# Attention with gate projections woven in: an output's addition ordered directly behind its copy, and the first gate's second half accumulated in the output's bank

## The chip, the core and the metric

The kernel runs on one core of one Trainium2 chip. The metric is the time of one execution on the device in microseconds; the median of several executions counts. Beside it there is one profiled execution, from which all rows of the trace in this document come. The engines are called as the profile calls them: PE is TensorE's matmuls, PEld its weight loads, DVE is VectorE, ACT is ScalarE, POOL is GpSimd, SP is SyncE.

## The reference

One transformer block over 1024 tokens of width 1024, in float32. The input is normalized and modulated, and one wide projection gives queries, keys and values of 8 attention heads, the streams of a recurrent branch (RWKV-7), and two gates of 1024 columns. Attention has a causal mask and a decay that is summed along the sequence:

```python
logits = einsum('bhqd,bhkd->bhqk', q, k) * scale + cum[..., :, None] - cum[..., None, :]
probs  = softmax(where(causal, logits, -inf))
o_fox  = einsum('bhqk,bhkd->bhqd', probs, v)
gate_fox, gate_rwkv = split(sigmoid(p_gate), 2, axis=-1)
merged = gate_fox * (o_fox @ fox_w_out) + gate_rwkv * (o_rwkv @ rwkv_w_out)
h = h + gate1 * (merged @ w_o)
```

A second half of the block, a gated feed-forward network with a short convolution, and a last normalization follow. The change touches only the stretch in which attention is computed, together with the last part of the gate projection `p_gate`.

## The kernel before

The work runs in stages: modulation and normalization, the recurrent branch with the projections beside it, attention, the two branch projections, the output projection, and the feed-forward network. To keep nearly float32 precision, a large product is done as three products of values that are split into a high and a low part (`hi`, `lo`).

**The planner.** In the recurrent stage and in attention the order of TensorE's instructions is written out by a small planner in Python, `Weave`. It keeps a clock of its own, `weave.now`, in nanoseconds, which every matmul advances by a fixed cost (a gate matmul of 512 columns costs 512 / 2.4 = 213), and one clock for ScalarE and one for VectorE, which `use(engine, after, cost)` advances. The work that matters is written as chains (generators) that issue instructions and then yield how long to wait. `run` takes the chain that is due, with spawned chains first. If none is due, `fill` issues matmuls of the filler, one at a time, until the next chain is due. The filler of the attention stage are the late gates: of the 16 gate tiles of 128 columns, those that are left when attention begins. While `weave.hold` lies ahead of the clock, no filler is issued.

In this stage the orders on TensorE, VectorE and ScalarE are the order in which the chains issue the instructions. Each of these engines works through its queue in that order, waiting where an operand isn't ready. The queues of SP and POOL, which carry the weight loads, the casts of late weights to their high part, and the loads of the heads, are ordered by the tile framework.

**Attention.** `s_chain` begins at 10,500 on the planner's clock, when the first head is expected to be loaded; until then only filler is issued. For a head `h` and a pair of row blocks `I` it issues logits into bank pairs `lg`. `softmax` takes the negated maximum (VectorE, line 1049), the exponential with its sum (ScalarE, 1053), the reciprocal and the scaling (VectorE, 1058 and 1059). `t_chain` transposes the probabilities (`tp`), `halve` splits them into `th` (ScalarE, 1086) and `tl` (VectorE, 1089), and `a_chain` multiplies them by the values into `ov_ps`, half of the only output bank. The high and the low part of the values give two halves of 64 rows there.

**`collect`** empties the output bank, once for every head and `I`, 32 times. ScalarE copies one half of the rows (line 1120). The chain yields until the planner's clock is past that copy, and only then is VectorE's addition of the other half issued (line 1122). So whatever other chains issue on VectorE in between comes ahead of the addition. `ov_free` then tells `a_chain` when the bank is free again.

**`late_gate`** issues a gate tile as two halves of 512 columns, 24 matmuls each, both into the one bank `rk_ps`. After a half it sets `weave.hold` and spawns `gate_out`, which reads the bank twice on ScalarE (Abs and Relu, lines 1162 and 1163), sets the hold anew to the planned end of these, and finishes the sigmoid in SBUF with two more activations, an addition and an exponential (1165 to 1170). The second half of the last gate stays in the bank and is read out after the stage.

Of the kernel before, what the change touches and what calls it, by code (L numbers as in the profile page):

```python
# [9 lines left out]
F32 = mybir.dt.float32  # L10
F32R = mybir.dt.float32r
AF = mybir.ActivationFunctionType
# [6 lines left out]
NH = 512  # L19
# [113 lines left out]
def hybrid_block(ctx: ExitStack, tc: tile.TileContext, a, out):  # L133
    nc = tc.nc
    weave = Weave()
    ctx.enter_context(tc.manual_schedule(engines={mybir.EngineType.PE}))

    def mm(o, lhsT, rhs, start, stop, more=False):

        weave.mm_cost(o, lhsT, rhs)  # L140
        nc.tensor.matmul(o, lhsT, rhs, start=start, stop=stop, skip_group_check=more)  # L141
# [5 lines left out]
    def f32(ap):  # L147
        return ap.bitcast(F32)
# [95 lines left out]
    marks = {}  # L244
    late_lo = deque()

    def lower(wait=0):

        yield wait
        if late_lo:  # L250
            hi, lo, raw = late_lo.popleft()
            for c in range(0, 1024, NH):
                tt(lo[:, c : c + NH], raw[:, c : c + NH], f32(hi[:, c : c + NH]), op=ALU.subtract)
            weave.use("DVE", weave.now, 1300)
# [30 lines left out]
    def gemm_steps(ps, w, x, cs, nk=KT, w0=0, by_kt=False):  # L285
        (wh, wl), (xh, xl) = w, x
        order = [(i, kt) for i in range(3) for kt in range(nk)]
        if by_kt:
            order.sort(key=lambda o: o[1])
        for n, (i, kt) in enumerate(order):  # L290
            ww, xx = ((wh, xh), (wh, xl), (wl, xh))[i]
            k0 = (w0 + kt) * 128
            mm(ps, ww[:, k0 : k0 + 128], xx[:, kt, cs], start=n == 0, stop=n == len(order) - 1)
            yield
# [27 lines left out]
    u = (u_hi, u_lo)  # L322
# [4 lines left out]
    def gate_steps(w, i, pps, ptag, pool, tag):  # L327
        if weave.late == 1:
            yield from late_gate(w, i)
            return  # L330
        for hf in range(2):
            cs = slice(hf * NH, hf * NH + NH)
            ps = pps.tile([128, NH], F32, tag=ptag, name=f"gt{i}_{hf}")
            yield from gemm_steps(ps, w, u, cs)

            g = pool.tile([128, NH], F32, tag=tag, name=f"gs{i}_{hf}")
            nc.scalar.activation(g, ps, AF.Abs)
            nc.scalar.activation(g, g, AF.Exp, scale=-1.0)
            nc.scalar.activation(g, g, AF.Ln, bias=1.0)
            stt(g, ps, 0.0, g, op0=ALU.min, op1=ALU.subtract)  # L340
            nc.scalar.activation(g, g, AF.Exp)
            nc.sync.dma_start(d_gate[i, :, cs], g)


    pb = ctx.enter_context(tc.tile_pool(name="pb", bufs=2, space=PS))
    with ExitStack() as es:
# [66 lines left out]
        with tc.tile_pool(name="st", bufs=1) as st, tc.tile_pool(name="stp", bufs=2, space=PS) as stp, \  # L413
# [24 lines left out]
            def mod_load(i, tags):  # L438
                ws = [st.tile([128, D], F32, tag=tags[kt % len(tags)], name=f"wm{i}{kt}", bufs={"mw": 4, "xt": 8}[tags[kt % len(tags)]])
                      for kt in range(KT)]  # L440
                for kt, w in enumerate(ws):
                    nc.sync.dma_start(w, a["w_mod"][kt * 128 : kt * 128 + 128, i * D : i * D + D])
                return ws, st.tile([128, D], F32, name=f"acc{i}")
# [69 lines left out]
            m = [mod_load(1, ("mw",)), None]  # L513
# [496 lines left out]
    with tc.manual_schedule(engines={mybir.EngineType.DVE, mybir.EngineType.Activation}):  # L1010
        seq = [(h, I) for h in range(8) for I in ((0, 1, 3, 2) if h == 7 else (3, 0, 2, 1))]
        lg_free, tp_free, pl_free, ps_free, th_free, ov_free = (deque([0.0] * n) for n in (2, 2, 4, 2, 3, 1))
        probs, av_queue, halves = {}, deque(), {}
        ov_ps = pb.tile([128, NH], F32, tag="big", name="ov")[:, 0:256]
        rk_ps = pb.tile([128, NH], F32, tag="big", name="rk_ps")

        def slot(free):
# [76 lines left out]
        def a_chain():  # L1094

            for _ in range(8 * 10):
                while not av_queue:
                    yield 100
                t, h, I, jj, th, tl = av_queue.popleft()
                yield t - weave.now  # L1100
                if jj == 0:
                    yield from slot(ov_free)
                vh = heads[h][2]
                order = [(0, th), (1, th), (1, tl), (0, tl)] if jj == I else [(0, th), (0, tl), (1, th), (1, tl)]
                for x, (k, t) in enumerate(order):
                    o0 = 128 if (jj == I and k == 1) else 0
                    mm(ov_ps[:, o0:256], vh[:, 2 * jj + k, :], t[:, 256 * k : 256 * k + 256 - o0],
                       start=jj == 0 and x == 0, stop=jj == I and x == 3)
                th_free.append(weave.now + 260)
                if jj == I:  # L1110
                    weave.spawn(collect(h, I), 260)
                yield 0

        def collect(h, I):
            p, hf, oc = h // 2, I // 2, slice(I % 2 * 256, I % 2 * 256 + 256)
            rows = slice(h % 2 * 64, h % 2 * 64 + 64)
            if (p, hf) not in halves:
                halves[p, hf] = at.tile([128, NH], F32, tag="o", name=f"o{p}{hf}"), []
            o, got = halves[p, hf]
            nc.scalar.copy(o[rows, oc], ov_ps[rows, :])  # L1120
            yield weave.use("ACT", weave.now, 270) + 140 - weave.now
            tt(o[rows, oc], o[rows, oc], ov_ps[64 - h % 2 * 64 : 128 - h % 2 * 64, :], op=ALU.add)
            t = weave.use("DVE", weave.now, 340) + 140
            ov_free.append(t + 70)
            got.append(I)
            if len(got) == 4:
                cs = slice(hf * NH, hf * NH + NH)
                if h < 7:
                    nc.gpsimd.tensor_copy(fx[0][p][:, cs], o)
                    nc.gpsimd.tensor_tensor(fx[1][p][:, cs], o, f32(fx[0][p][:, cs]), op=ALU.subtract)  # L1130
                    return
                yield t - weave.now
                nc.scalar.copy(fx[0][p][:, cs], o)
                yield weave.use("ACT", weave.now, 530) + 140 - weave.now
                tt(fx[1][p][:, cs], o, f32(fx[0][p][:, cs]), op=ALU.subtract)
# [4 lines left out]
        def late_gate(w, i):  # L1140
            while any(x[1] is w[1] for x in late_lo):
                for _ in lower():
                    pass
            for hf in range(2):
                cs = slice(hf * NH, hf * NH + NH)
                yield from gemm_steps(rk_ps, w, u, cs)
                if i == 15 and hf == 1:

                    marks["rest"] = rk_ps
                    return  # L1150
                weave.hold = weave.now + 1000
                pending.append((i, hf))
                weave.spawn(gate_out(i, hf, cs), 260)
                yield

        def gate_out(i, hf, cs):

            n = marks["gate"] = marks.get("gate", 0) + 1
            g = (at.tile([128, NH], F32, tag="gs", name=f"gs{i}_{hf}", bufs=1) if n % 3 == 1 else
                 gsp.tile([128, NH], F32, tag="sp0", name=f"gs{i}_{hf}"))  # L1160
            m = at.tile([128, NH], F32, tag="gm", name=f"gm{i}_{hf}", bufs=1)
            nc.scalar.activation(g, rk_ps, AF.Abs)
            nc.scalar.activation(m, rk_ps, AF.Relu, scale=-1.0)
            weave.hold = weave.use("ACT", weave.now, 960) + 210
            nc.scalar.activation(g, g, AF.Exp, scale=-1.0)
            nc.scalar.activation(g, g, AF.Ln, bias=1.0)
            yield weave.use("ACT", weave.now, 960) + 140 - weave.now
            tt(g, g, m, op=ALU.add)
            yield weave.use("DVE", weave.now, 600) + 140 - weave.now
            nc.scalar.activation(g, g, AF.Exp, scale=-1.0)  # L1170
            weave.use("ACT", weave.now, 480)
            nc.sync.dma_start(d_gate[i, :, cs], g)
            pending.remove((i, hf))
# [12 lines left out]
    def bank(k, name):  # L1186
        return pb.tile([128, NH], F32, tag="big", name=name) if k > 5 else pz.tile([128, NH], F32, tag=f"p{k}", name=name)
# [34 lines left out]
    if "rest" in marks:  # L1222
        g, m = (gsp.tile([128, NH], F32, tag="sp0", name=f"rest{k}") for k in range(2))
        i = nc.scalar.activation(g, marks["rest"], AF.Abs)
# [405 lines left out]
    ps = {t: [bank(k, f"wo{t}_{c}") for c, k in enumerate(ks)] for t, ks in enumerate(((0, 5), (6, 7), (1, 2)))}  # L1630
# [12 lines left out]
    def wo_do(t, k):  # L1643
        ps = [bank(k + c, f"wo{t}_{c}") for c in range(2)]
        for kt in range(KT):
            wo_mm(t, kt, ps)
        return ps

    ps = wo_do(3, 3)
# [7 lines left out]
    ps = wo_do(4, 0)  # L1657
# [15 lines left out]
    for t, k in ((5, 2), (6, 6), (7, 4)):  # L1673
        ps = wo_do(t, k)
# [229 lines left out]
    for s, k in enumerate(ORDER):  # L1904
        ps = banks[4:] if k in (7, 4, 2) else banks[0:4]
        own = NP - 4 if s == 6 else NP
        for j in range(own):
            u = s * NP + j
# [106 lines left out]
```

## Time and profile before

| | |
|---|---|
| Runs | 1660.62, 1658.31, 1658.08 us; median 1658.31 |
| Profiled execution, its own time | 1662.01 us |
| Span from its first to its last instruction | 1660.2 us |
| Mean granted TensorE clock | 0.989 |
| Gate matmuls into `rk_ps` | from 622.4 us on |
| First and last addition of `collect` (line 1122) | 653.4 and 827.4 us |
| First matmuls of the branch projections | 829.09 us |

A row of the trace gives start and duration in microseconds, the engine, the line, the operation, the tile written and the tiles read (buffer numbers left out), the shape, and the number of instructions merged in the row. In brackets stands how long the engine was idle before it, and whose end released it. Most matmuls have line 141 and most transposes line 145, since helpers issue them; they are told apart by their tiles. A row of a table by stretch gives the busy time of each engine in that stretch and the granted clock, 1.00 being full speed.

### The profile page before, as it was taken

The page shows a single profiled execution, that of the slowest core. Times are in us where ns is not written, and L with a number is a line of the kernel's source. Part 1 is how long each engine was busy: PE and PEld are TensorE (multiplying, and loading weights), DVE is VectorE, ACT ScalarE, POOL GpSimd, SP SyncE. Part 2 cuts the span into 40 slices and gives each one's busy share as a digit, 9 for nine tenths or more (in the row PEclk, how much of TensorE's full clock was granted, in tenths as well). Part 3 has the DMA queues.
Part 4 walks back from the last instruction along what each step waited for, and adds up shares of the span by engine and source line. Part 5 has one row for each costly group of instructions (what it writes and reads, how often), then busy time and mean ns, then how long its engine had stood idle before and what let it go on. Part 6 is the DMA issues. An engine that isn't in the chain of part 4 may idle for free.

```text
span 1660.2 us, 25947 instructions
## 1 busy us (share of the span) xinstructions
PE 1615.2 (97%) x9694; PEld 1346.1 (81%) x9694; DVE 1223.2 (74%) x2371; ACT 822.3 (50%) x1540; POOL 130.3 (8%) x152
## 2 busy tenths in 40 slices
PE   7999999999999999999999999999999999999998
PEld 7777777898978788888778887888888888888886
DVE  5786787878876536888678347897777777786677
ACT  5563335444455656666623225654444444555455
POOL 0011001111111011221022000000000000000000
PEclk9999999999999999999999999999999999999999
DMA  8488645443343246433187411243223223574363
GB/s 336 139 322 238 177 116 140 131 121 97 100 115 97 96 129 153 124 114 110 64 323 265 166 70 58 66 138 108 96 95 120 97 96 108 208 266 156 125 209 108
DMA packets 121645, 240.59 MB, mean 145 GB/s; under 512 B 40048, under 2 KB 48880, under 8 KB 121520
## 3 DMA queue, kind: packets, MB, share of 16 engines
q1 hardware_dynamic: 113040, 220.58, 40.7%
q0 software_dynamic: 8480, 18.37, 4.2%
q8 instruction: 76, 1.25, 0.3%
q14 instruction: 49, 0.40, 0.1%
HBM read 173.35 MB, written 65.54 MB: 144 GB/s over the span
## 4 chain that ended last, share of the span: by engine, by line
PE 62%; DVE 3%; ACT 2%; DMA 1%; issue 1%; SPq 0%; ACTq 0%; DVEq 0%
PE X L141 14%; PE D L141 13%; PE Y L141 7%; PE wo L141 5%; PE br L141 5%; PE gt L141 4%; PE rk_ps L141 4%; PE W L141 3%; PE lg L141 2%; PE ov L141 2%; PE tp L145 2%; DVE nm L1049 1%; DVE P L1059 1%; DMA g<-d_gate 0%; DVE tl L1089 0%
## 5 line engine op out<-in xcount | busy, mean ns | idle before, releaser
L141 PE MATMUL D<-op,op 128*128 128x512 f32 x924 | 209.8, 389 | 0.0
L141 PEld LDWEIGHTS D<-op,op 128*128 128x128 f32 x924 | 173.3, 188 | 36.3 <-DVE op L1252 0.3
L141 PE MATMUL X<-T_m,S 128*128 128x512 f32 x440 | 106.9, 389 | 0.0
L141 PEld LDWEIGHTS X<-T_m,S 128*128 128x128 f32 x440 | 82.5, 188 | 17.5 <-ACT x L1542 0.4
L1251 ACT CAST op<-g 128x512 fp32r<-128x512 f32 x77 | 47.8, 621 | 72.1 <-PE D L141 47.8
L1252 DVE TENSOR_TENSOR op<-g,op 128x512 fp32r<-128x512 f32 x77 | 53.0, 688 | 41.1 <-ACT op L1251 41.1
L1502 DVE SCALAR_TENSOR_TENSOR c<-ab,vec,c 128x512 f32<-128x512 f32 x88 | 65.9, 749 | 18.4 <-ACT c L1505 16.8
L784 DVE TENSOR_TENSOR t<-E,M 128x60 f32<-128x60 f32 (+24 forms) x248 | 56.1, 226 | 26.6 <-DMA M<-sm 20.6
L274 DVE TENSOR_TENSOR lo_in<-raw_in,hi_in 128x512 fp32r<-128x512 f32 x84 | 57.7, 725 | 22.0 <-PE gt L141 7.2
L1466 DVE TENSOR_TENSOR A<-ur,A 128x512 fp32r<-128x512 f32 x64 | 43.9, 688 | 39.0 <-ACT A L1462 38.8
L1466 DVE TENSOR_TENSOR S<-ur,S 128x512 fp32r<-128x512 f32 x66 | 45.5, 691 | 35.2 <-ACT S L1462 35.1
L1462 ACT CAST S<-ur 128x512 fp32r<-128x512 f32 x66 | 41.0, 622 | 56.1 <-DVE ur L1455 30.9
L141 PE MATMUL Y<-T_h,S 128*128 128x512 f32 x264 | 65.6, 398 | 1.6 <-ACT T_h L1720 1.0
L141 PE MATMUL Y<-T_h,A 128*128 128x512 f32 x264 | 63.4, 389 | 0.0
L1053 ACT ACTIVATE P<-lg,nm 128x896 f32<-128x896 f32 (+3 forms) x64 | 47.4, 742 | 29.3 <-DVE nm L1049 19.6
L141 PEld LDWEIGHTS Y<-T_h,S 128*128 128x128 f32 x264 | 50.6, 192 | 13.4 <-ACT T_h L1720 1.8
L1462 ACT CAST A<-ur 128x512 fp32r<-128x512 f32 x64 | 39.6, 621 | 42.9 <-PE X L141 31.0
L141 PE MATMUL W<-B_f,A 128*128 128x512 f32 x252 | 60.6, 389 | 0.0
L786 DVE TENSOR_TENSOR E<-E,t 128x60 f32<-128x60 f32 (+24 forms) x248 | 55.8, 225 | 6.4
L141 PE MATMUL X<-B_b,A 128*128 128x512 f32 x252 | 60.5, 389 | 0.0
L141 PEld LDWEIGHTS Y<-T_h,A 128*128 128x128 f32 x264 | 49.5, 188 | 10.3
L272 ACT CAST hi_in<-raw_in 128x1024 fp32r<-128x1024 f32 x42 | 43.9, 1049 | 25.4 <-PE ps_rkv L141 11.3
(481 smaller groups left out, 4142.0 us busy)
## 6 DMA issues: line engine op xcount, KB each, us to landing
raw_in<-in_w_in SPq DMA_DIRECT2D x50, 512.0 KB, 3.9
wm<-in_w_mod SPq DMA_DIRECT2D x48, 512.0 KB, 6.7
ur<-in_w_up SPq DMA_DIRECT2D x44, 512.0 KB, 4.0
g<-d_g SPq DMA_DIRECT2D x35, 512.0 KB, 3.8
d_g<-gs SPq DMA_DIRECT2D x44, 256.0 KB, 2.0
d_g<-c SPq DMA_DIRECT2D x33, 256.0 KB, 4.3
d_st<-qh SPq DMA_DIRECT2D x64, 128.0 KB, 2.4
stA<-d_st POOLq DMA_DIRECT2D x8, 1024.0 KB, 6.2
```

Of the source, the lines that this page charges most:

```text
L141: nc.tensor.matmul(o, lhsT, rhs, start=start, stop=stop, skip_group_check=more)
L145: nc.tensor.transpose(o, i, eye)
L272: nc.scalar.copy(hi, raw)
L274: nc.vector.tensor_tensor(lo[:, c : c + NH], raw[:, c : c + NH], f32(hi[:, c : c + NH]), op=ALU.subtract)
L784: tt(tv, E32[:, 0:J, s : s + 1].to_broadcast([128, J, W]), M32[:, s : s + 1, s + 1 : 32].to_broadcast([128, J, W]), op=ALU.mult)
L786: tt(E32[:, 0:J, s + 1 : 32], E32[:, 0:J, s + 1 : 32], tv, op=ALU.add)
L1053: nc.scalar.activation(e[:, 0:n], lg[:, 0:n], AF.Exp, bias=nm[:, 0:1], accum_out=nm[:, 1:2])
L1251: nc.scalar.copy(hi, src)
L1252: tt(lo, src, f32(hi), op=ALU.subtract)
L1462: nc.scalar.copy(hi, src)
L1466: tt(lo, src, f32(hi), op=ALU.subtract)
L1502: stt(c, ab[:, x + hf * NH : x + hf * NH + NH], V("conv_w", 22 * x + i), c, op0=ALU.mult, op1=ALU.add)
```

## The change

There are two edits.

In `collect` the chain no longer yields between the copy and the addition. The addition is issued directly behind the copy, its cost is booked on VectorE's clock from the copy's planned end on, and the chain yields afterwards, until the addition's planned end. Then it reports the bank as free.

In `late_gate` the first gate of the stage (no gate has been counted in `marks` yet) sends its second half into the output's bank, whose whole 512 columns now have a name, `ov_bank`. For this gate no hold is set, neither by `late_gate` nor by `gate_out`, so filler goes on at once. `gate_out` gets the bank that it reads as an argument. All other gates are as before.

```diff
-        ov_ps = pb.tile([128, NH], F32, tag="big", name="ov")[:, 0:256]
+        ov_bank = pb.tile([128, NH], F32, tag="big", name="ov")
+        ov_ps = ov_bank[:, 0:256]
...
             nc.scalar.copy(o[rows, oc], ov_ps[rows, :])
-            yield weave.use("ACT", weave.now, 270) + 140 - weave.now
+            t = weave.use("ACT", weave.now, 270) + 140
             tt(o[rows, oc], o[rows, oc], ov_ps[64 - h % 2 * 64 : 128 - h % 2 * 64, :], op=ALU.add)
-            t = weave.use("DVE", weave.now, 340) + 140
+            t = weave.use("DVE", t, 340) + 140
+            yield t - weave.now
             ov_free.append(t + 70)
...
+            first = "gate" not in marks
             for hf in range(2):
                 cs = slice(hf * NH, hf * NH + NH)
-                yield from gemm_steps(rk_ps, w, u, cs)
+                ps = ov_bank if first and hf else rk_ps
+                yield from gemm_steps(ps, w, u, cs)
...
-                weave.hold = weave.now + 1000
+                weave.hold = weave.now if first else weave.now + 1000
                 pending.append((i, hf))
-                weave.spawn(gate_out(i, hf, cs), 260)
+                weave.spawn(gate_out(i, hf, cs, ps, first), 260)
...
-        def gate_out(i, hf, cs):
+        def gate_out(i, hf, cs, ps, first):
...
-            nc.scalar.activation(g, rk_ps, AF.Abs)
-            nc.scalar.activation(m, rk_ps, AF.Relu, scale=-1.0)
-            weave.hold = weave.use("ACT", weave.now, 960) + 210
+            nc.scalar.activation(g, ps, AF.Abs)
+            nc.scalar.activation(m, ps, AF.Relu, scale=-1.0)
+            t = weave.use("ACT", weave.now, 960) + 210
+            weave.hold = weave.hold if first else t
```

## The prediction

> **What bounds the kernel now.** I read the page first, then a table of busy time by stretch, and then went through the attention stage in order of time on all engines.
>
> ```profile
> span 1660.2 us, 25947 instructions
> PE 1615.2 (97%) x9694; PEld 1346.1 (81%) x9694; DVE 1223.2 (74%) x2371; ACT 822.3 (50%) x1540; POOL 130.3 (8%) x152
> ...
> 645.00:805.00 160.00, 154.34 (x973) 135.66 (x972) 136.24 (x279) 109.26 (x255) 29.20 (x34) 0.99 0.39 109
> ```
>
> TensorE is busy for 97% of the span, and in the 160 us that make up most of the attention stage for 154.34. So there are two ways to gain: shorten an idle piece of TensorE, or take something off it. The change takes nothing off, so every gain has to be an idle piece that disappears. VectorE is close behind: 136.24 of 160 us, so 23.8 us of it are free. ScalarE has 109.26. The stage begins with gate matmuls that fill TensorE until the first head can start, and here is its first idle piece:
>
> ```profile
> 624.22 1.98 PE L141 MATMUL rk_ps<-u_lo,hi_in 128*128 128x512 f32 x8
> 626.03 1.98 PE L141 MATMUL rk_ps<-u_hi,lo_in 128*128 128x512 f32 x8
> 628.04 0.60 ACT L1162 ACTIVATE gs<-rk_ps 128x512 f32<-128x512 f32 x1 [1.39 <-PE rk_ps L141]
> 628.53 0.59 ACT L1163 ACTIVATE gm<-rk_ps 128x512 f32<-128x512 f32 x1
> 629.18 2.11 PE L141 MATMUL rk_ps<-u_hi,hi_in 128*128 128x512 f32 x8 [1.18 <-ACT gm L1163]
> ...
> 632.94 0.84 PE L141 MATMUL rk_ps<-u_hi,lo_in 128*128 128x512 f32 x3
> ...
> 634.75 2.27 DVE L1049 TENSOR_REDUCE nm<-lg 128x1 f32<-128x896 f32 x2 [2.51 <-PE lg L141]
> ...
> 636.94 0.60 ACT L1162 ACTIVATE gs<-rk_ps 128x512 f32<-128x512 f32 x1
> ...
> 638.17 2.08 PE L141 MATMUL rk_ps<-u_hi,hi_in 128*128 128x512 f32 x8 [0.20 <-ACT gm L1163]
> ...
> 639.11 1.10 ACT L1053 ACTIVATE P<-lg,nm 128x1024 f32<-128x1024 f32 x1
> ```
>
> The first gate's first half ends, ScalarE takes Abs and Relu out of its bank, and TensorE stands still for 1.18 us because the second half wants the same bank. After the second half it waits another 0.20 us. The second half also hurts ScalarE: its four activations (636.94 to 639.11) run ahead of the exponential at 639.11, whose maximum was ready when the two reductions ended at 634.75 + 2.27 = 637.02. The first softmax thus starts 2.1 us late.
>
> The second edit concerns the copy and the addition that empty the output's bank, 32 times each. The first two rows are the group rows of that tile, then one place in order of time, then two lines of the table of waits (total us, times, longest):
>
> ```profile
> L1120 ACT COPY o<-ov x32: 352/367/370, 650.7 to 827.0; 64x256 f32<-64x256 f32 x32
> L1122 DVE TENSOR_TENSOR o<-o,ov x32: 416/420/424, 653.4 to 827.4; 64x256 f32<-64x256 f32 x32
> ...
> 677.28 0.37 ACT L1120 COPY o<-ov 64x256 f32<-64x256 f32 x1 [0.58 <-PE ov L141]
> 677.84 0.45 PE L141 MATMUL lg<-stB 68*128 68x512 f32 x1
> 678.16 0.68 DVE L1089 TENSOR_TENSOR tl<-tp,th 128x512 fp32r<-128x512 f32 x1
> 678.94 0.49 DVE L1059 TENSOR_SCALAR P<-P,nm 128x512 f32<-128x512 f32 x1
> 679.34 1.22 DVE L1049 TENSOR_REDUCE nm<-lg 128x1 f32<-128x1024 f32 x1
> 680.59 0.42 DVE L1122 TENSOR_TENSOR o<-o,ov 64x256 f32<-64x256 f32 x1
> 681.06 0.39 PE L141 MATMUL ov<-th,vh 128*128 128x256 f32 x1 [1.97 <-DVE o L1122]
> ...
> PE ov L141 <- DVE o L1122: 2.0, 1, 2.0
> DVE o L1122 <- ACT o L1120: 6.3, 5, 1.9
> ```
>
> The copy ends at 677.65, but its addition starts at 680.59: VectorE does a subtraction, a scaling and a maximum over 1024 columns first. TensorE waits 1.97 us for that addition, the only such wait of it in 32. And it pays again:
>
> ```profile
> 679.00:681.00 2.00, 0.09 (x1) 0.00 (x0) 1.97 (x3) 2.00 (x6) 0.00 (x0) 1.00 0.91 154
> 681.00:683.00 2.00, 1.94 (x13) 1.94 (x13) 1.92 (x5) 1.97 (x4) 0.00 (x0) 0.77 0.25 74
> 683.00:685.00 2.00, 2.00 (x10) 1.90 (x10) 1.90 (x4) 1.47 (x4) 0.00 (x0) 0.50 0.29 98
> 685.00:687.00 2.00, 2.00 (x15) 1.82 (x14) 0.71 (x4) 0.59 (x2) 1.81 (x2) 0.88 0.58 179
> 829.00:833.00 4.00, 3.92 (x17) 3.25 (x18) 1.35 (x3) 3.19 (x7) 2.54 (x2) 1.00 1.00 361
> ```
>
> (The columns are the stretch, its length, busy time of PE, PEld, DVE, ACT and POOL, then the granted TensorE clock, the DMA share and GB/s.) In the six microseconds behind this pause the clock falls to 0.77, 0.50 and 0.88. That is 2 x (0.23 + 0.50 + 0.12) = 1.70 us of full-speed time lost while TensorE was fully booked. Not every pause does that: the last row stands behind a pause of 1.84 us (its row is below) and shows 1.00.
>
> **The gate's second half in the other bank.** By the kernel's own bookkeeping a gate half takes 24 x 213 ns, so two halves without the hold fill 10.24 of the 10.5 us before the heads begin, and the next gate starts in the old bank, long empty. The pauses of 1.18 and 0.20 us have no cause left: -1.38 us. The rows show the same from the other side: 16 and 3 matmuls of the second half ran before the first logits, and now all 24 and two of the next do, seven more, at 1.81 us per eight (624.22 to 626.03) 1.58 us of filler. The output's bank is free for this: no output matmul has touched it yet, and the two activations that read it out come directly after the half's end at about 633, while the two reductions above end only at 637.02. So four gate activations leave the first softmax's way, up to 2.1 us for the whole chain of heads. From below, the gain can be eaten at the stage's end, where the same filler now covers waits:
>
> ```profile
> 824.79 1.76 PE L141 MATMUL rk_ps<-u_hi,lo_in 128*128 128x512 f32 x7
> 825.02 0.56 DVE L1089 TENSOR_TENSOR tl<-tp,th 128x384 fp32r<-128x384 f32 x1 [1.46 <-ACT th L1086]
> 826.39 0.34 PE L141 MATMUL ov<-th,vh 128*128 128x256 f32 x2
> ...
> 829.09 2.11 PE L141 MATMUL br<-fx,hi_br 128*128 128x512 f32 x8 [1.84 <-ACT hi_br L1214]
> ```
>
> Seven filler matmuls run here before the last output. If they have been used up earlier, the output could start when its operand is ready at 825.58, 0.8 us sooner, and the rest of 1.58 us becomes idle time. So the edit is worth 0.6 (1.38 - 0.78) to 2.1 us. I take 1.4: the chain also starts earlier, which speaks against the low end, but other work shares it, which speaks against the high one. The weights' loads and casts on SP's and POOL's queues are not moved past anything else; only the matmuls that free their buffers come up to 1.6 us sooner.
>
> **The addition directly behind its copy.** At the place above, the last logits matmul starts at 677.84. The kernel issues their maximum 351 ns of its own clock behind them, and a collection that falls due during a block of logits is issued right behind the block, so that the maximum (679.34) lands between the copy and the addition. In the new order the addition precedes at least that maximum: 1.25 us sooner (679.34 instead of 680.59), which leaves 0.7 us of the 1.97. If it also passes the subtraction and the scaling, the whole 1.97 goes. I take the sure part, 1.25 us. A pause of 0.7 us is shorter than the 1.18 us at 629.18, after which the table below shows no loss, so I let the clock's 1.70 us go too:
>
> ```profile
> 629.20:633.40 4.20, 4.20 (x19) 3.47 (x20) 1.90 (x3) 1.71 (x3) 0.17 (x1) 1.00 1.01 212
> ```
>
> [...]
>
> **What the second edit costs.** VectorE works in the written order, so an addition that waits for ScalarE holds all behind it: maxima, scalings and the subtractions whose results the next output matmuls read. What it costs is seen at a place like this one:
>
> ```profile
> 661.38 0.37 ACT L1120 COPY o<-ov 64x256 f32<-64x256 f32 x1
> 661.52 0.69 DVE L1089 TENSOR_TENSOR tl<-tp,th 128x512 fp32r<-128x512 f32 x1 [0.47 <-ACT th L1086]
> ...
> 662.24 0.42 DVE L1122 TENSOR_TENSOR o<-o,ov 64x256 f32<-64x256 f32 x1
> ...
> 736.24 0.39 PE L141 MATMUL ov<-tl,vh 128*128 128x256 f32 x1 [0.32 <-DVE tl L1089]
> 740.13 0.39 PE L141 MATMUL ov<-tl,vh 128*128 128x256 f32 x1 [0.76 <-DVE tl L1089]
> 816.31 0.38 PE L141 MATMUL ov<-tl,vh 128*128 128x256 f32 x1 [0.61 <-DVE tl L1089]
> ```
>
> With the addition first, VectorE would wait until the copy ends at 661.75 and lose 0.23 us against a start at 661.52. 32 times that is 7.4 us; the bounds are 0 (VectorE is late anyway, as at 677.65, where it lags the copy by 2.9 us) and 32 x 0.37 = 11.8 us, a whole copy each. The cover is VectorE's free 23.8 us in 160. What reaches TensorE is small now: 1.97 us for the addition, and 0.32 + 0.76 + 0.61 = 1.69 us for late subtractions. Below zero is possible as well, because those 1.69 us can go when the order is redrawn. I take +0.4 us, a twentieth of the 7.4, since TensorE finds filler planned for nearly every gap.
>
> **The sum.** -1.4 - 1.25 - 1.7 + 0.4 = -3.95 us. The profiled execution took 1662.01 us (1660.2 of span and 1.8 around it), which becomes 1658.1. It is 3.7 us above the median of the runs, 1658.31, and the slow clock may be part of that excess. Applied to the median, the forecast is 1654.4 us, with a range of its own from 1650.8 (all upper ends, 2.1 + 1.97 + 1.70, and the 1.69 us of subtractions: 7.5 us) to 1655.0.
>
> **Rivals.** First, the loss of clock is not bound to this pause, or not present in the runs that make the median. Then -1.4 - 1.25 + 0.4 = -2.25 us: 1656.1. [...] Against it, the dip follows the pause at once. Chance 0.13.
>
> Second, the edits do less than they say. The planner redraws the order of the whole stage, the addition that was late stays late behind VectorE's backlog (2.9 us, most of it work issued before the copy), and the filler spent early is missing at the end, which leaves -0.6 us: 1657.7. For it: the stage's seven filler matmuls above end at 826.55, when its last output matmuls begin (826.39), so there is none to spare. Chance 0.17.
>
> Third, VectorE becomes the bound, and the kernel is slower. Its place is the middle of the stage, where 85% of VectorE is taken and each held addition delays three kinds of work. If the 7.4 us of waits all come through, with a new late output in the place of the old one, only the first edit's 1.4 us stand against them: +6.0 us, 1664.3. It turns into a loss that can be measured once the 32 waits come to 4.7 us in the path, 0.15 us each. Its support is the row at 661.52; against it, five additions that waited already, 6.3 us in all, made TensorE wait hardly at all. [...] Chance 0.21.
>
> **How the numbers follow.** The forecast has 0.49. I count 0.2% (3.3 us) as what a measurement of this kernel can tell from no change, so faster means under 1655.0 and slower over 1661.6. The forecast lies below, the first two rivals between, the third above: 0.49, 0.30 and 0.21. The range goes from 1650.8 up to 1663.0, past the point where the third rival begins, and leaves out about its upper half and a few in a hundred below.
>
> **What would show it.** In the changed profile, rk_ps and the output's bank should take the first 48 gate matmuls without a pause, seven more than now should stand before the first logits, and the second exponential should start near 637. The wait of an output matmul for L1122's successor should be under 1 us and the clock in that place 1.00. VectorE's idle time before the 32 additions, 6.3 us now, should grow to somewhere between 8 and 14 us. The prediction is wrong if TensorE's waits for subtractions, maxima or scalings grow by several us, if a new pause with its loss of clock shows up, or if TensorE stands idle at the end of the stage for lack of filler.

## The result: 0.25% slower

| | before | after |
|---|---|---|
| Median of 22 runs each, side by side | 1658.19 us (1655.87 to 1664.01) | 1662.15 us (1659.06 to 1667.59) |
| Ratio to before | | 1.0025, 95% interval 1.0016 to 1.0033 |
| Profiled execution, its own time | 1662.01 us | 1661.97 us |
| Mean granted clock of the profiled execution | 0.989 | 0.993 |

The change costs 4.0 us. The two profiled executions took the same time, because that of before lies 3.8 us above this median; so the totals of the two traces say nothing, and the stages have to be read.

First the page of after and its table by stretch (length, busy time of PE, PEld, DVE, ACT and POOL, granted clock, DMA share, GB/s):

```profile
span 1660.2 us, 25934 instructions
PE 1610.0 (97%) x9694; PEld 1340.8 (81%) x9694; DVE 1221.2 (74%) x2371; ACT 823.1 (50%) x1540; POOL 133.9 (8%) x152
...
645.00:805.00 160.00, 154.43 (x977) 135.78 (x976) 133.46 (x277) 108.31 (x251) 31.50 (x34) 1.00 0.37 110
665.00:685.00 20.00, 19.59 (x119) 17.09 (x120) 15.78 (x33) 14.59 (x34) 2.87 (x4) 1.00 0.44 114
828.80:833.00 4.20, 4.11 (x11) 3.27 (x12) 1.56 (x3) 3.39 (x7) 2.52 (x2) 0.59 0.96 337
```

The middle of the stage looks as good as before: TensorE is busy for 154.43 of 160 us and the clock is full where it had fallen to 0.50. But behind the stage's end the clock is 0.59 now, where it was 1.00. Those 4.2 us lose 4.2 x 0.41 = 1.72 us, as much as the old place had lost. The start of the stage, in order of time:

```profile
625.37 1.98 PE L141 MATMUL rk_ps<-u_hi,lo_in 128*128 128x512 f32 x8
627.18 1.98 PE L141 MATMUL ov<-u_hi,hi_in 128*128 128x512 f32 x8
...
630.81 1.98 PE L141 MATMUL ov<-u_hi,lo_in 128*128 128x512 f32 x8
632.62 0.62 PE L141 MATMUL rk_ps<-u_hi,hi_in 128*128 128x512 f32 x2
...
633.07 0.39 PE L141 MATMUL lg<-stA 128*128 128x512 f32 x1
...
637.06 1.12 ACT L1054 ACTIVATE P<-lg,nm 128x1024 f32<-128x1024 f32 x1
```

The second half goes into `ov` with no pause, 50 gate matmuls stand before the first logits, and the second exponential starts at 637.06 instead of 639.11: the first edit does here what it was to do. Next, the waits of the stage (total us, times, longest). In before, VectorE waited 6.3 us in 5 additions for ScalarE's copies, and TensorE waited 2.0 us for the late addition and at two more kinds of work of VectorE, in all 2.0 + 1.7 + 0.2 = 3.9 us:

```profile
PE ov L141 <- DVE tl L1089: 1.7, 3, 0.8
PE tp L145 <- DVE nm L1058: 0.2, 1, 0.2
```

In after:

```profile
DVE o L1123 <- ACT o L1121: 14.4, 17, 1.7
PE ov L141 <- DVE tl L1090: 2.8, 6, 0.9
PE br L141 <- ACT hi_br L1219: 2.1, 1, 2.1
PE lg L141 <- DVE nm L1050: 1.5, 1, 1.5
PE ov L141 <- DVE o L1123: 1.3, 3, 0.6
PE tp L145 <- DVE tl L1090: 0.7, 1, 0.7
```

The late addition has gone from 2.0 to at most 0.6 us a time. In its place stand late subtractions (`tl`), a late maximum (`nm`, 1.5 us at one place) and the additions: 2.8 + 1.5 + 1.3 + 0.7 = 6.3 us. The end of the stage:

```profile
816.55 1.99 PE L141 MATMUL rk_ps<-u_hi,lo_in 128*128 128x512 f32 x8
826.32 0.50 PE L141 MATMUL ov<-tl,vh 128*128 128x128 f32 x2
828.89 3.61 PE L141 MATMUL br<-fx,hi_br 128*128 128x512 f32 x8 [2.08 <-ACT hi_br L1219]
```

The filler is used up at 818.5, 8 us before the last output ends. The eight branch matmuls take 3.61 us, at a granted clock of 0.53 (828.89 to 832.50), against 2.11 before.

### The profile page after: what moved, and what is told of

It is laid out like the page before. It is cut to its first block, busy times and chain, and to the rows that moved or that the text cites. A ratio compares the mean times of both kernels' runs of the same rounds, so it can differ in the third digit from the quotient of the medians.

```text
span 1660.2 us, 25934 instructions
## 1 busy us (share of the span) xinstructions
PE 1610.0 (97%) x9694; PEld 1340.8 (81%) x9694; DVE 1221.2 (74%) x2371; ACT 823.1 (50%) x1540; POOL 133.9 (8%) x152
## 3 DMA queue, kind: packets, MB, share of 16 engines
q8 instruction: 76, 1.25, 0.3%
## 4 chain that ended last, share of the span: by engine, by line
PE 64%; DVE 4%; ACT 2%; issue 1%; DMA 0%; ACTq 0%; DVEq 0%
PE X L141 14%; PE D L141 13%; PE Y L141 7%; PE gt L141 5%; PE wo L141 5%; PE br L141 5%; PE W L141 3%; PE rk_ps L141 3%; PE ov L141 2%; PE lg L141 2%; PE tp L145 1%; PE ps_rkv L141 1%; DVE tl L1090 1%; DVE nm L1050 1%; DVE P L1060 1%
```

## The experiments

Each kernel was timed in five rounds beside the kernel before. "Stage" is the time in its profile from the first late gate matmul to the 13th branch matmul, taken at full clock: what the clock lost in it, the sum of (1 - granted clock) over stretches of 1 us, is subtracted. For before it is 209.55 - 1.71 = 207.84 us, for after 211.60 - 1.71 = 209.89 us. "Pauses" are TensorE's waits for VectorE in the stage: 3.9 and 6.3 us.

**How sure a ratio is.** The kernel before, once more.

> The kernel before itself, to learn what its executions have in common: the span and granted clock of each, and a second profile. If the pause of 1.97 us in front of 681.06 and the clock of 0.50 behind it belong to the kernel, both stand in this profile too, and the clock lost there is part of the median. If the pause stays and the clock does not fall, the 1.70 us that the forecast took for it was not there to be gained. Time: the same as before, within 0.1%.

Ratio 0.9995 (0.9986 to 1.0005), with the same pause (1.98 us) and the same fall of the clock in the same place. So 0.1% is what five rounds can tell apart.

**Each edit alone.** Two kernels: the direct addition with the old gate code, and the new gate code with the old `collect`.

```diff
# one edit alone: only the first, or only the second, of these
+            t = weave.use("ACT", weave.now, 270) + 140
             tt(o[rows, oc], ...)
...
+                ps = ov_bank if first and hf else rk_ps
```

> Only the addition directly behind its copy; the first gate as before. Theory of the held queue (the additions that wait for ScalarE slow the chain of heads, and with it the stage): slower than before by 4 to 6 us, with VectorE idle ahead of the additions for 12 us or more, against 6.3 before. Theory of the spent filler (the time is lost at the stage's end, because the filler was used up early by the first gate's two banks): within 1 us of before, since no filler is moved to the front.

> Only the first gate's second half in the output's bank; the addition as before. Held queue: faster than before by 1 to 2 us, the pause of 1.18 us gone and attention ahead by about 2 us, nothing set against it. Spent filler: slower by 2 to 4 us, with the last filler matmul several us ahead of the last output and a clock near 0.6 in the first 4 us of the branch projections.

The addition alone: 1.0027 (1.0016 to 1.0038), stage 212.5 us, pauses 6.6 us. The gate alone: 1.0013 (1.0002 to 1.0024), stage 209.7 us, pauses 5.5 us. Neither edit gained. The addition alone came out as the theory of the held queue had told, with 21.6 us of idle time of VectorE before the additions; the gate alone lost about what the theory of the spent filler had told, though its last filler ended only 2.3 us ahead of its last output. But in each the planner had redrawn the whole stage, so these two runs mix the edit with a new order. The gate alone, for example, ran into a new late subtraction:

```profile
789.72 0.39 PE L141 MATMUL ov<-tl,vh 128*128 128x256 f32 x1 [1.85 <-DVE tl L1090]
```

**Is the first edit's early start given back by late heads, or by missing filler?** The heads were let in 1.5 us sooner by the planner's clock, the last eight gate matmuls were kept until the last output was issued, or both.

```diff
-            yield 10500
+            yield 9000
...
# and / or, in late_gate and before the last drain:
+                    if i == 15 and hf == 1 and n == 15:
+                        weave.hold = 1e9
...
+        weave.hold = weave.now
```

> Both edits, and the chain of the heads begins at 9,000 on the planner's clock, not at 10,500, so that seven filler matmuls less are spent ahead of it and seven more are left for the end. Spent filler: the end is covered again, the clock stays at 1.00 there, and the kernel is 2 to 4 us faster than with both edits alone, so about as fast as before. Held queue: the stage stays as slow against its own start, and only the 1.5 us of the earlier start are gained.

> Both edits, and the last eight filler matmuls (the last third of the last gate half) are held back until the last output has been issued, so that they stand in the pause of 2.08 us ahead of the branch projections. If that pause is what drops the clock at the stage's end: clock 1.00 behind it, and the stage 1 to 2 us shorter than with both edits alone (211.6 us from the first late gate matmul to the third group of branch matmuls), unless the eight matmuls are missed in the gaps before. If the drop comes from the thin last 8 us as a whole, the clock still falls, perhaps earlier, and nothing is gained.

> Both edits, heads from 9,000 on, last eight filler matmuls held. If the three causes add (held additions, filler spent early, clock drop): 1 to 2 us faster than the same kernel without the hold, which was as fast as before, so 0.05 to 0.15% faster than before. If the early start already took what there was, the same as before.

> The first gate's edit alone, heads from 9,000 on, last eight filler matmuls held; the addition as before. Held queue: without the waits of VectorE this is the fastest of all, 2 to 4 us faster than before. Spent filler alone: about like the same kernel with the addition moved.

> The kernel before, with the heads from 9,000 on and nothing else. It is a control: no operation, bank or addition is changed, only the planner's order is drawn anew. If order alone scatters the stage by microseconds, its time without the loss of clock (207.8 us in both profiles of the kernel before) moves by 1 us or more either way. If not, it is 0 to 1.5 us faster for the earlier start, and the 2 to 5 us that the single edits cost are theirs.

| kernel | ratio | stage, full clock |
|---|---|---|
| both edits, heads earlier | 0.9994 (0.9982 to 1.0006) | 207.4 |
| both edits, filler held | 1.0018 (1.0007 to 1.0029) | 209.1 |
| both edits, earlier and held | 0.9994 (0.9984 to 1.0003) | 206.0 |
| gate edit, earlier and held | 1.0000 (0.9991 to 1.0009) | 207.5 |
| before, heads earlier | 1.0010 (0.9999 to 1.0021) | 207.5 |

With the filler held, the pause at the end of the stage shrank from 2.08 to 0.26 us and the clock stayed full there:

```profile
831.53 2.14 PE L141 MATMUL br<-fx,hi_br 128*128 128x512 f32 x8 [0.26 <-ACT hi_br L1223]
```

Its ratio does not differ from that of after beyond the intervals, and a fall of the clock showed up at 856, behind the stage. So missing filler explains at most a part of the 4 us: with the filler held the medians still lie 2.4 us apart. Earlier heads bring both edits back to before's time, while before itself does not profit (1.0010). How slow the new order is thus depends on how the planner fits it together; a change of 1.5 us in one constant is worth as much as the whole effect under study. To learn what an edit costs, the order has to be held fast.

**The addition moved, in before's own order.** TensorE's and ScalarE's instructions are those of before, one by one. On VectorE the addition is issued with its copy; 27 of the 32 thereby come earlier.

```diff
-            yield weave.use("ACT", weave.now, 270) + 140 - weave.now
             tt(o[rows, oc], ...)
+            yield weave.use("ACT", weave.now, 270) + 140 - weave.now
```

> The kernel before, in its own order on TensorE and ScalarE, instruction by instruction; only on VectorE 27 of the 32 additions stand directly behind what was issued before their copy. The planner books as before, so nothing else is drawn anew. Theory of the held queue (VectorE waits for ScalarE and comes late to everything behind): slower than before by 2 to 4 us, VectorE idle ahead of the additions for 12 us or more against 6.3, TensorE waiting 3 us more for VectorE in all. Theory of the redrawn order (the additions cost next to nothing themselves; the planner's new order of the whole stage does): within 1 us of before, and the pause of 1.97 us at the late addition is gone or shorter, with the clock kept there.

Ratio 1.0025 (1.0014 to 1.0037), medians 1663.60 against 1659.02 us, stage 213.4 us: as slow as after, with no other difference than the place of 27 additions. Its waits, and the place of the prediction in order of time:

```profile
DVE o L1121 <- ACT o L1120: 19.9, 23, 2.5
PE ov L141 <- DVE tl L1089: 4.1, 6, 1.2
PE tp L145 <- DVE tl L1089: 2.4, 3, 1.1
PE tp L145 <- DVE P L1059: 1.1, 2, 0.8
PE ov L141 <- DVE o L1121: 0.8, 1, 0.8
```

```profile
676.86 0.37 ACT L1120 COPY o<-ov 64x256 f32<-64x256 f32 x1 [0.58 <-PE ov L141]
679.05 0.42 DVE L1121 TENSOR_TENSOR o<-o,ov 64x256 f32<-64x256 f32 x1
679.50 1.23 DVE L1049 TENSOR_REDUCE nm<-lg 128x1 f32<-128x1024 f32 x1
679.52 0.39 PE L141 MATMUL ov<-th,vh 128*128 128x256 f32 x1 [0.85 <-DVE o L1121]
...
682.16 0.50 PE L141 MATMUL ov<-tl,vh 128*128 128x128 f32 x2 [0.81 <-DVE tl L1089]
...
683.09 0.37 ACT L1120 COPY o<-ov 64x256 f32<-64x256 f32 x1
683.49 0.42 DVE L1121 TENSOR_TENSOR o<-o,ov 64x256 f32<-64x256 f32 x1 [0.79 <-ACT o L1120]
...
685.88 0.63 PE L145 MATMUL tp<-cst,P 128*128 128x128 f32 x4 [1.01 <-DVE tl L1089]
```

The wait of 1.97 us shrinks to 0.85: the addition now precedes the maximum (679.50), as predicted. But 2.6 us later an output matmul waits 0.81 us for its subtraction, which stands behind the maximum and a scaling on VectorE, and until 683.49 VectorE itself stands for 0.79 us until the next copy ends, after which the transposes wait 1.01 us for a subtraction held behind it. One pause of 1.97 us has become three of 2.67 us. In the whole stage VectorE's idle time before additions goes from 6.3 to 19.9 us, and TensorE's waits for VectorE from 3.9 to 4.1 + 2.4 + 1.1 + 0.8 = 8.4 us.

**The reverse: after's order, additions back where they stood.** TensorE and ScalarE as in after; the same with heads earlier and filler held; and after itself beside them.

```diff
-            t = weave.use("ACT", weave.now, 270) + 140
+            t0 = weave.use("ACT", weave.now, 270) + 140
+            t = weave.use("DVE", t0, 340) + 140
+            yield t0 - weave.now
             tt(o[rows, oc], ...)
-            t = weave.use("DVE", t, 340) + 140
             yield t - weave.now
```

> Both edits' order on TensorE and ScalarE, instruction by instruction, but on VectorE the additions stand where they stood before the change, behind what is issued until their copy's planned end. Held queue: 2 to 4 us faster than both edits, so about as fast as before. Redrawn order: as slow as both edits, within 1 us.

> Both edits, heads from 9,000 on, the last eight filler matmuls held, and the additions moved back on VectorE alone. Held queue: 1 to 3 us faster than the same kernel with held additions, whose stage took 206.0 us: the fastest of all, 0.1 to 0.2% faster than before. Redrawn order: no change against that kernel.

> Both edits once more, beside the other three on the same chip, for the comparison within one call and for a second profile. 3 to 4 us slower than before. If the loss of clock at a place belongs to the order of the instructions, this profile shows it again at the stage's end and nowhere else in the stage. [...]

After again: 1.0026 (1.0013 to 1.0038), which repeats the result. With the additions moved back: 1.0051 (1.0034 to 1.0068, six runs), so in this order the direct addition is the better one, and what costs the 4 us in after's own order is not isolated by taking it back. The waits show why:

```profile
PE ov L141 <- DVE o L1125: 7.9, 7, 2.4
DVE o L1125 <- ACT o L1121: 5.7, 7, 1.6
```

VectorE's idle time falls from 14.4 to 5.7 us, as it should, but seven output matmuls now wait 7.9 us for the bank. The planner had written TensorE's order for a bank that comes free directly behind the copy. In the version with earlier heads the additions moved back make no difference that shows: 0.9995 (0.9983 to 1.0007) against 0.9994.

**The bank alone, in before's order.** TensorE's order and the planner's books are before's; only the bank of the first gate's second half is another. Then the same with the last eight filler matmuls held, and a third, with the filler held as well, in which one single addition, that of the late place, is issued with its copy.

```diff
+                ps = ov_bank if first and hf else rk_ps
...
# second and third kernel, also:
+                    if i == 15 and hf == 1 and n == 15:
+                        weave.hold = 1e9
...
# third kernel, also (tt_ issues the addition):
+            if (h, I) == (1, 0):
+                tt_()
             yield weave.use("ACT", weave.now, 270) + 140 - weave.now
+            if (h, I) != (1, 0):
+                tt_()
```

> The kernel before in its own order, instruction by instruction; only the first gate's second half is accumulated in the output's bank, while the planner books its holds as before. If the bank itself is harmless and the first edit's loss was the redrawn order: 1.4 us less, 0.05 to 0.1% faster than before, with the pauses of 1.18 and 0.20 us gone and the pause of 1.97 us at the late addition still there. If the bank costs something: as slow as the first edit alone, 0.1% slower.

> The same, and the last eight filler matmuls are held until the last output has been issued (seven of them stood in the last gaps, one behind the outputs already). The pause of 1.84 us ahead of the branch projections should shrink to about 0.3 us, while the last outputs come 0 to 0.8 us sooner: 1 to 2 us faster than the same kernel without it. If the gaps before the last outputs only grow by what the end gains, no change.

> The same, and one of the 32 additions, the one that TensorE waits 1.97 us for (second head, first pair of row blocks), stands directly behind its copy; the other 31 as before. Held queue: one addition in the right place gives 1 us (1.97 to about 0.85) without the price of the other 26, and the drop of the clock behind it goes. In all 0.15 to 0.3% faster than before. If the chain behind it is late anyway, the same as without it.

The bank alone: 0.9993 (0.9983 to 1.0003), stage 206.3 us, that is 1.5 us shorter; in the time the gain is not clear of the interval. With the filler held: 0.9989 (0.9979 to 0.9999), stage 205.5 us, 1658.06 against 1660.07 us. This is the only version that is faster than before beyond its interval, and only just; of so many versions one may do that by chance. With one addition moved as well: 0.9993 (0.9983 to 1.0002), stage 206.6 us. Both edits together in before's order were not run; the medians of the two alone add up to 4.6 - 1.3 = 3.3 us, near the 4.0 of after. Two rows of the first and three of the third:

```profile
627.02 1.98 PE L141 MATMUL ov<-u_hi,hi_in 128*128 128x512 f32 x8
678.71 0.39 PE L141 MATMUL ov<-th,vh 128*128 128x256 f32 x1 [1.98 <-DVE o L1123]
```

```profile
678.59 0.39 PE L141 MATMUL ov<-th,vh 128*128 128x256 f32 x1 [0.84 <-DVE o L1122]
681.23 0.50 PE L141 MATMUL ov<-tl,vh 128*128 128x128 f32 x2 [0.79 <-DVE tl L1090]
689.51 0.39 PE L141 MATMUL ov<-th,vh 128*128 128x256 f32 x1 [0.65 <-DVE o L1122]
```

The gate's bank takes its pause away without touching anything else. The one addition gives up 1.98 us for 0.84 + 0.79 + 0.65 = 2.28. Even at the place for which the second edit was best suited it does not shorten the stage.

**How the 4 us divide.** Each timed run comes with its mean clock. Within one kernel the time is longer where the clock is lower: over all these groups of runs, 0.001 of mean clock goes with 0.84 us (the pooled slope of time against clock; in after's second set of 12 runs the correlation is -0.94). Applied to the difference between two kernels this gives an estimate. After's second set has a mean of 0.9902 against 0.9922 of before, which makes 1.6 of its 4.3 us (difference of means), and leaves 2.7 us for the order; the stage in the two profiles of after is 2.05 and 1.5 us longer than before's at full clock. In after's first set the clock was 0.9918, so the share of the clock is itself uncertain. For the addition moved in before's order the clock was higher than before's (0.9933), and 5.5 us are left for the place of the additions, with a stage 5.5 us longer.

## Why the prediction was wrong

The forecast was 1654.4 us; measured was 1662.15, inside the range but on the other side of before's time. The third rival, VectorE as the bound through held additions, comes closest, with +4.0 us where it said +6.0. Its mechanism is shown in before's order; how much of after's 4.0 us it makes, beside the redrawn order, no run separates. Step by step:

- **The gate's second half, -1.4 us: right by itself, lost in the new order.** With before's order the stage is 1.54 us shorter. With the edit as it was made, the planner's clock at the start changes and everything behind it is redrawn. Of the attention matmuls, 116 instead of 98 had begun at 660 us, but 297 against 296 at 700, and 761 against 762 at 800. The prediction saw that the order would be redrawn, and took at most 0.8 us off the edit, for filler missing at the end. It costs more: alone, with its redrawn order, the edit is 0.13% slower, which is 2.2 us. Why that order has 5.1 us of waits for subtractions is not settled.
- **The late addition, -1.25 us: right in size, wrong as a gain.** The wait went from 1.97 to 0.85 us when only the addition moved, 1.12 us. Then the work that it passed was late instead.
- **The held additions, +0.4 us: the step that failed.** VectorE's extra wait came out nearly as the rows at 661.38 had said (8 to 14 us of idle time were told, 14.4 were measured), and was 13.6 us more in before's order. Wrong was the share of a twentieth that reaches TensorE. In before's order TensorE's waits for VectorE rise by 4.5 us, although the late addition gives 1.1 us back; so at least 5.6 of 13.6 us arrive, four tenths, and the kernel is 4.6 us slower with nothing else changed. The reason given for the small share, filler planned for nearly every gap, does not hold: the filler stands at fixed places in TensorE's order, here those of before, and TensorE waited for late subtractions (4.1 + 2.4 us in nine waits) although more filler stood behind them. Gate matmuls ran beside 14 of VectorE's 23 waits there (in before, beside two of its five); it was the subtractions behind the held additions that came late, as in the rows at 682.16 and 685.88. And the 23.8 us in which VectorE was free were no cover, as they weren't free at the moment when a subtraction was due.
- **The clock, -1.7 us: the place was right, the gain was none.** The fall behind 681 went with its pause. Another came behind the pause of 2.08 us at the end of the stage, of the same size. The first rival said that the loss isn't bound to this pause; in all four profiles with before's order and this pause it was there (0.50 from 682.06 us on in before, from 679.0 and 678.9 on in the bank alone, without and with the filler held). But pauses of 1.84, 1.94 and 2.03 us brought none (below), so it is not shown that the whole 1.7 us was bound to this pause.
- **Missing filler at the end** (in the second rival) was there, 8 us before the end of the last output. Holding eight matmuls back made the pause vanish, but the time of after only moved from 1.0025 to 1.0018, within the intervals.

Of the told signs, the pauses at the start, the seven more matmuls, the exponential at 637, the wait under 1 us with a full clock and, but for 0.4 us, the idle time of VectorE came as told. They were signs that the edits do their work, and none of them measures what the work costs. The signs that would make it wrong came too, all three: waits for subtractions and maxima, a new pause with its loss of clock, and an end of the stage without filler.

## What to carry to other kernels

An instruction moved forward in an in-order queue has to be priced by what it holds back when its operand is late, in the rows of those instructions and of who waits for them, not by the average free time of the engine: at 683.49 one addition waited 0.79 us for its copy, and TensorE then 1.01 us for a subtraction behind it, though VectorE was free for 27.6 of 160 us there (645 to 805, 132.39 busy). Where a planner writes the order, test an edit with the other engines' order held fast before testing it as it would be used: here that told the bank, which costs nothing (0.9993), and the moved additions, which cost 0.25%, apart; the redrawn orders had mixed them. Do not book a fall of the clock as time to be won with one pause, since another pause can take its place, as that of 2.08 us did here for that of 1.97.

## What the runs showed of the hardware

Which pause the clock falls behind is less simple than the prediction had it. Pauses of TensorE in this stage with a fall of the clock behind them: 1.97 and 1.98 us (before, twice, and the bank alone; 0.50 from 682.06 on in before), 2.08 (after, 0.53 over the eight matmuls behind it, and each edit alone), 2.39 (the additions moved back, 0.66 from 771 to 776), 1.85 (the gate alone, at 789.72), 1.84 (the addition moved in before's order, at the end of the stage, 0.72 from 830.5 to 836.5), 1.27 and 1.38 (the addition alone, at 792 and 823). Pauses without one: 1.84 (before, at 829.09, 1.00 from 829 to 833), 1.94 (before with heads earlier, 1.00 from 654 to 660), 2.03 (the gate edit with heads earlier, 1.00 from 680 to 686). Two rows behind such pauses, the first of the gate edit with heads earlier, behind 2.03 us, the second of the addition moved in before's order, behind 1.84 us:

```profile
680.00:686.00 6.00, 4.52 (x33) 4.25 (x34) 5.43 (x12) 5.89 (x14) 0.00 (x0) 1.00 0.60 185
```

```profile
830.50:836.50 6.00, 4.17 (x11) 3.30 (x12) 2.47 (x4) 4.68 (x9) 2.53 (x2) 0.72 1.02 355
```

The second loses 6 x 0.28 = 1.7 us. Nearly every fall seen in the stage lost about 1.7 us, which is 3.4 us at 0.50. Length alone does not decide, since 1.84 us stands in both lists. Here is before at the pause that ends at 681.06, the 3.41 us ahead of the fall and the 3.41 us that it lasts:

```profile
678.65:682.06 3.41, 1.44 (x10) 1.01 (x10) 3.28 (x8) 3.38 (x8) 0.00 (x0) 1.00 0.75 127
682.06:685.47 3.41, 3.41 (x17) 3.22 (x16) 2.86 (x6) 2.86 (x6) 0.36 (x1) 0.50 0.28 96
```

The fall comes 1.0 us behind the end of the pause, when TensorE is fully busy again. Nor does every fall have a pause ahead of it: in after the clock is 0.51 from 938.25 to 941.65, behind 3.40 us (934.80 to 938.20) in which the profile calls TensorE busy throughout, mostly with matmuls of one column (32 in a row from 933.73 on). What decides was not tried by an experiment and is not shown here.

After's second profile lost twice as much behind the same 2.08 us pause as its first (3.41 against 1.71 us), so even one kernel differs from run to run: there the fall began at 830.37, inside the pause, and the clock stayed at 0.50 for 6.8 us.
